# Factors per token spread to rows by way of DRAM instead of by transposes, in a two-layer hybrid encoder trunk

## The chip, the cores and the metric

The kernel runs on one NeuronCore of a Trainium2 chip. The metric is the device time of one execution in microseconds (us). The kernel before takes 1721.14 us, the median of three runs (1721.01 to 1721.66). Its engines are named as in the profile: PE is TensorE's matmul, PEld its weight load, DVE is VectorE, ACT ScalarE, POOL GpSimd, SP the sync engine, which here only issues DMAs.

## The reference

Two residual layers run on a sequence of 512 tokens of width 1024, in float32. Cut to what matters here, one layer is:

```
xn = rms_norm(x, norm1_g)                       # one factor per token
aq, ak, av, bq, bk, bv, cq, ck, cv, cg, gates = split(xn @ w_in)
ya = dilated_mixer(...)      # 6 heads in 3 groups; group outputs weighted by softmax over the
                             # groups' log-denominators: one weight per token, head and group
yb = diff_attention(...)     # 4 heads of 128 values
yb = rms_norm(yb, b_out_norm_g) * (1 - lam_init)          # one factor per token and head
yc = bidirectional_retention(...)                          # 4 heads of 128 values
yc = silu(cg) * rms_norm(yc, c_out_norm_g)                 # one factor per token and head
merged = sum_i sigmoid(gate_i) * (branch_i @ W_branch_i)
x = x + merged @ w_o
h = square(relu(rms_norm(x, norm2_g) @ w_mlp1))            # one factor per token
x = x + h @ w_mlp2
```

Every product with a weight matrix is made in three passes of a 32-bit matmul format: each operand is split into a high and a low part, and high by high, high by low and low by high are added.

## The kernel before, in words

**Layout.** Activations lie feature-major: a tile has 128 features on the partitions and the 512 tokens along the row. Projections to queries, keys and values come out token-major (128 tokens on the partitions, four such blocks, `NJ = 4`). A factor per token is worked out token-major, as a column of a tile of 128 partitions by 4 blocks. To multiply a feature-major tile it has to stand in every partition as a row of 512.

**The stages.** Each layer runs `sequence` (L841): projection waves A, B and C, gates G, branch products W, output products O, and then M1 and M2, the two MLP products. `gemm` (L287) does one chunk of 512 (or 384) output columns in four accumulators `acc0` to `acc3`, one PSUM bank each, with weights that SP fetches (`raw`), ACT rounds (`whi`) and DVE completes (`wlo`), two units ahead of use. Attention, retention and norms run as side threads between the matmuls of the projections. Four more PSUM banks (`pm`) serve all of these.

**The four places where a factor is spread.** (1) `norm_spread` (L423) turns a column broadcast to 128 x 128 through TensorE, four blocks, into a bank `ps_norm`, and ACT copies that to the row tile `rB`. It runs twice a layer. (2) `head_norm` (L579) runs for the four differential heads (branch 1) and the four retention heads (branch 2). It turns the feature-major head `y` to token-major (`ps_yt`, four transposes), ACT squares and sums it, DVE works out the factor `hg` and multiplies (`yn`), and four more transposes bring `yn` back to feature-major in `ps_yb`, from where it is scaled and split. (3) `thread_a` (L709) has the group weights `wt` (`awt`, 24 columns: 3 groups x 2 heads x 4 blocks). For each group DVE copies 8 of them out to 128 x 512 (`wx`), TensorE turns that (`ps_thread_a`), and DVE multiplies the group's output `ya` by the bank.

**What sets the order.** The methods only record operations, in program order. `emit` (L1064) then places them engine by engine by a list schedule of its own: each operation has a reckoned duration, each hand-over a reckoned delay, and the earliest ready one goes first. A DMA from POOL is reckoned as 1.0 us of POOL and 2.0 us until it has landed:

```
d = kb / 290 if name == "SP" else 0.1 if name == "ACT" else 1.0    # L233, in dma()
far = 2.0 if i in self.moves else BEHIND[e]                        # L1168, in emit()
```

On the chip every engine then works through its own instructions strictly in that order and waits where an input has not come. `yield ("wait", "yb")` (L603) and `("wait", "wx")` (L750) hold a side thread back by 8.0 and 1.0 us of reckoned TensorE time while operations are recorded. POOL does nothing else but issue DMAs: it loads the residual `xr` (L958) and stores `xspill` (L1006).

Of the kernel before, what the change touches and what calls it, by code (L numbers as in the profile page):

```python
# [9 lines left out]
FT = mybir.dt.float32  # L10
FR = mybir.dt.float32r
AF = mybir.ActivationFunctionType
OP = mybir.AluOpType
# [3 lines left out]
P = 128  # L17
SEQ = 512
D = 1024
NJ = 4  # L20
# [92 lines left out]
class Trunk:  # L113
# [307 lines left out]
        return r  # L421

    def norm_spread(self, r):  # L423
        b2 = self.ps(name="ps_norm")
        for j in range(NJ):
            self.tr(b2[:, j * P:(j + 1) * P], r[:, j:j + 1].to_broadcast([P, P]), self.ident)
        rB = self.U(name="rB")
        self.act(rB, b2)
        return rB


    def wave_buffers(self, kind):
# [146 lines left out]
    def head_norm(self, l, branch, h, y, s):  # L579
        gain = self.ghead[:, 2 * (branch - 1) + l:2 * (branch - 1) + l + 1]  # L580
        if branch == 2:
            yield ("need", ("cg", l))
        yield ("wait", "y")
        b = self.ps(name="ps_yt")
        for j in range(NJ):
            self.tr(b[:, j * P:(j + 1) * P], y[:, j * P:(j + 1) * P], self.ident)
        ss = self.tiny(4, "yss")
        for j in range(NJ):
            self.act(y[:, j * P:(j + 1) * P], b[:, j * P:(j + 1) * P], AF.Square, accum_out=ss[:, j:j + 1])
        f = self.tiny(4, "hf")  # L590
        if s is not None:
            q = self.tiny(4, "hq")
            s0 = s.rearrange("p (j m) -> p j m", m=2)[:, :, 0]
            self.stt(q, s0, EPS, s0, OP.mult, OP.mult)
            self.stt(f, ss, 1.0 / 128, q, OP.mult, OP.add)
        else:
            self.ts(f, ss, 1.0 / 128, EPS, OP.mult, OP.add)
        g = self.tiny(4, "hg")
        self.rsqrt(g, f)
        yn = self.U(name="yn")  # L600
        self.tt(yn.rearrange("p (j e) -> p j e", j=NJ), b.rearrange("p (j e) -> p j e", j=NJ),
                g[:, :, None].to_broadcast([P, NJ, P]), OP.mult)
        yield ("wait", "yb")  # L603
        b2 = self.ps(name="ps_yb")
        for j in range(NJ):
            self.tr(b2[:, j * P:(j + 1) * P], yn[:, j * P:(j + 1) * P], self.ident)
        out = self.y[l, branch]
        if branch == 1:
            out[h] = self.split(b2, "yn", scale=gain)
        else:  # L610
            self.stt(yn, b2, gain, self.silu[l][h], OP.mult, OP.mult)
            self.silu[l][h] = None
            yield
            out[h] = self.split(yn, "yn")
        if None not in out:
            self.flags.add(("y", l, branch))
        yield
# [91 lines left out]
    def thread_a(self, l):  # L709
        nmx = self.tiny(24, "anm", 2)  # L710
        den = self.tiny(24, "aden", 2)
        ys = []
# [19 lines left out]
        d = self.tiny(24, "ad", 2)  # L732
        for g in range(3):
# [8 lines left out]
        wt = self.tiny(24, "awt", 2)  # L742
        self.tt(wt.rearrange("p (g a) -> p g a", a=8), d.rearrange("p (g a) -> p g a", a=8),
                z1[:, None, :].to_broadcast([P, 3, 8]), OP.mult)
        yield
        for g in range(3):
            wx = self.U((P, NJ, 2, 64), name="wx")
            self.copy(wx, wt[:, g * 8:g * 8 + 8].rearrange("p (m j) -> p j m", j=NJ)[:, :, :, None].to_broadcast(
                [P, NJ, 2, 64]))
            yield ("wait", "wx")  # L750
            b = self.ps(name="ps_thread_a")
            for j in range(NJ):
                self.tr(b[:, j * P:(j + 1) * P], wx[:, j].rearrange("p m d -> p (m d)"), self.ident)
            self.tt(ys[g], ys[g], b, OP.mult)
            yield
            self.y[l, 0].append(self.split(ys[g], "yn"))
            yield
# [461 lines left out]
```

## Time and profile before

| what | value |
|---|---|
| median of 3 runs | 1721.14 us (1721.01 to 1721.66) |
| the profiled execution, its own time | 1721.42 us |
| span, first to last instruction | 1719.6 us |
| PE busy | 1709.5 us, 99% of the span, 8120 matmuls |
| DVE, ACT, POOL busy | 1094.3 (64%), 813.0 (47%), 13.3 us (1%) |
| granted TensorE clock over the span | 1.000 |
| DMA queue of SP, of POOL | 26.0% and 1.0% of the 16 DMA engines' time |

The span leaves 1.8 us of the execution's own time outside. The profile page lists busy time by engine, the granted clock, DMA queues, the chain of work that ended last, and the costliest groups of instructions. A row of a timeline is: start in us, duration in us, engine, line, operation, output<-inputs, shape, count, and in brackets the idle time before it and who ended it. Matmuls overlap, so what one of them costs is read from the distance between starts and not from its duration.

### The profile page before, as it was taken

The numbers are of one execution on the slowest core, as the hardware profiler recorded it, in microseconds if no ns is written. First come the engines' busy times: TensorE is split into PE (matmuls) and PEld (weight loads), VectorE is DVE, ScalarE is ACT, GpSimd is POOL, SyncE is SP. The second block draws the span as 40 slices with busy tenths as digits, with TensorE's granted clock in tenths as the row PEclk, the third lists the DMA queues.
The fourth block names the chain that finished last, engine by engine and source line by source line (L and its number), as shares of the span: only waits on it lengthen the run. The fifth ranks groups of instructions, "written<-read, shape, count | busy, mean of one in ns | idle before, by whom it ended". The sixth has DMA issues, their size and how long they took to land. (4 is left out here: it accounts for less than half of the span.)

```text
span 1719.6 us, 21537 instructions
## 1 busy us (share of the span) xinstructions
PE 1709.5 (99%) x8120; PEld 1454.8 (85%) x8120; DVE 1094.3 (64%) x2126; ACT 813.0 (47%) x1529; POOL 13.3 (1%) x29
## 2 busy tenths in 40 slices
PE   8999999999999999999999999999999999999999
PEld 8889988888888888888898899888888888888887
DVE  8788897887655343434468788888867543434342
ACT  7676674655344232323457666646543441414141
POOL 0000000000000000000000000000000000000000
PEclk9999999999999999999999999999999999999999
DMA  6212212223322222222332222222232222222221
GB/s 222 106 60 72 83 56 95 78 74 105 104 98 98 98 98 98 98 95 93 107 123 86 71 68 78 80 74 86 74 123 90 96 97 98 98 98 98 98 92 68
DMA packets 47960, 160.64 MB, mean 93 GB/s; under 512 B 5616, under 2 KB 6256, under 8 KB 47728
## 3 DMA queue, kind: packets, MB, share of 16 engines
q1 hardware_dynamic: 45072, 151.84, 26.0%
q0 software_dynamic: 1920, 6.29, 1.0%
q8 instruction: 64, 1.05, 0.2%
q10 hardware_dynamic: 864, 1.13, 0.2%
q14 instruction: 40, 0.33, 0.1%
HBM read 155.05 MB, written 4.19 MB: 93 GB/s over the span
## 5 line engine op out<-in xcount | busy, mean ns | idle before, releaser
L185 DVE TENSOR_TENSOR wlo<-raw,whi 128x1024 fp32r<-128x1024 f32 (+2 forms) x297 | 345.0, 1162 | 456.7 <-ACT whi L175 456.0
L175 ACT ACTIVATE whi<-raw 128x1024 fp32r<-128x1024 f32 (+2 forms) x297 | 300.2, 1011 | 629.8 <-PE acc L224 560.7
L224 PE MATMUL acc<-xgh,whi 128*128 128x512 f32 x960 | 377.1, 393 | 0.0
L224 PE MATMUL acc<-xgl,whi 128*128 128x512 f32 x960 | 374.7, 390 | 0.0
L224 PE MATMUL acc<-xgh,wlo 128*128 128x512 f32 x960 | 374.2, 390 | 0.0
L224 PEld LDWEIGHTS acc<-xgh,wlo 128*128 128x128 f32 x960 | 180.3, 188 | 37.6
L224 PEld LDWEIGHTS acc<-xgh,whi 128*128 128x128 f32 x960 | 180.3, 188 | 37.4 <-DVE gate L194 0.8
L224 PEld LDWEIGHTS acc<-xgl,whi 128*128 128x128 f32 x960 | 180.4, 188 | 36.1
L224 PE MATMUL acc<-whi,xgh 128*128 128x384 f32 (+1 forms) x576 | 202.5, 355 | 6.0 <-ACT whi L175 5.5
L224 PE MATMUL acc<-wlo,xgh 128*128 128x384 f32 (+1 forms) x576 | 201.7, 350 | 0.0
L224 PE MATMUL acc<-whi,xgl 128*128 128x384 f32 (+1 forms) x576 | 201.3, 349 | 0.0
L224 PE MATMUL acc<-hh,whi 128*128 128x512 f32 x512 | 199.2, 389 | 0.0
L224 PE MATMUL acc<-hl,whi 128*128 128x512 f32 x512 | 199.2, 389 | 0.0
L224 PE MATMUL acc<-hh,wlo 128*128 128x512 f32 x512 | 199.2, 389 | 0.0
L224 PEld LDWEIGHTS acc<-whi,xgh 128*128 128x128 f32 x576 | 108.8, 189 | 13.0 <-ACT whi L175 5.8
L224 PEld LDWEIGHTS acc<-wlo,xgh 128*128 128x128 f32 x576 | 109.2, 189 | 6.0 <-DVE wlo L185 0.3
L224 PEld LDWEIGHTS acc<-whi,xgl 128*128 128x128 f32 x576 | 109.0, 189 | 5.3
L224 PEld LDWEIGHTS acc<-hl,whi 128*128 128x128 f32 x512 | 96.1, 188 | 20.0
L224 PEld LDWEIGHTS acc<-hh,wlo 128*128 128x128 f32 x512 | 96.1, 188 | 19.9
L224 PEld LDWEIGHTS acc<-hh,whi 128*128 128x128 f32 x512 | 96.1, 188 | 19.9
L175 ACT ACTIVATE qk<-ps_prep 64x512 fp32r<-64x512 f32 (+1 forms) x144 | 69.8, 485 | 20.3 <-DVE qk L185 11.4
L185 DVE TENSOR_TENSOR xr<-xr,acc 128x512 f32<-128x512 f32 (+1 forms) x81 | 54.6, 678 | 30.6 <-PE acc L224 30.1
(199 smaller groups left out, 2225.3 us busy)
## 6 DMA issues: line engine op xcount, KB each, us to landing
raw<-in_weights_dram SPq DMA_DIRECT2D x236, 512.0 KB, 3.2
raw<-in_weights_dram SPq DMA_DIRECT2D x55, 384.0 KB, 3.0
xt<-in_x_dram SPq DMA_DIRECT2D x8, 256.0 KB, 5.1
xr<-in_x_dram POOLq DMA_DIRECT2D x8, 256.0 KB, 3.9
xspill<-xr POOLq DMA_DIRECT2D x8, 256.0 KB, 2.5
xr<-xspill POOLq DMA_DIRECT2D x8, 256.0 KB, 3.5
blob<-in_blob_dram SPq DMA_DIRECT2D x1, 1024.0 KB, 8.4
raw<-in_weights_dram SPq DMA_DIRECT2D x4, 256.0 KB, 2.6
```

Of the source, the lines that this page charges most:

```text
L175: lambda: self.nc.scalar.activation(out, in_, func, **k))
L185: self.dve(out, [out], [a, b], lambda: self.nc.vector.tensor_tensor(out, a, b, op=op))
L224: self.op("PE", d, [out], [lhsT, rhs], lambda: self.nc.tensor.matmul(out, lhsT, rhs, start=start, stop=stop))
```

## The change

A helper `spread` takes a column tile, stores it to a scratch tile in DRAM as rows (a store of `n * 512` single elements of 4 bytes, from POOL's queue), and loads each row from DRAM into all 128 partitions (or two rows into 64 partitions each), again from POOL's queue. `norm_spread` uses it in place of four transposes and ACT's copy. `head_norm` multiplies the feature-major `y`, which it keeps, by the row tile `yr`, so that the four transposes back (`ps_yb`) go; the squares are written to the PSUM bank, since `y` must survive. `thread_a` stores all 24 weight columns at once (6 rows) and loads three tiles `wx` by six loads.

```diff
     def norm_spread(self, r):
-        b2 = self.ps(name="ps_norm")
-        for j in range(NJ):
-            self.tr(b2[:, j * P:(j + 1) * P], r[:, j:j + 1].to_broadcast([P, P]), self.ident)
-        rB = self.U(name="rB")
-        self.act(rB, b2)
-        return rB
+        return self.spread(r, 1, "rB")[0]
+
+    def spread(self, r, n, name, rows=P):
+
+        d = self.dp.tile([n, SEQ], FT, name=self.uid("row"))
+        self.dma(self.nc.gpsimd, d.rearrange("i (j p) -> p (i j)", j=NJ), r, 2)
+        out = []
+        for i in range(0, n, P // rows):
+            t = self.U(name=name)
+            for h in range(P // rows):
+                v = d[i + h]
+                self.dma(self.nc.gpsimd, t[rows * h:rows * h + rows], bass.AP(tensor=v.tensor, offset=v.offset, ap=[[0, rows], [1, SEQ]]), 256)
+            out.append(t)
+        return out
...
         for j in range(NJ):
-            self.act(y[:, j * P:(j + 1) * P], b[:, j * P:(j + 1) * P], AF.Square, accum_out=ss[:, j:j + 1])
+            self.act(b[:, j * P:(j + 1) * P], b[:, j * P:(j + 1) * P], AF.Square, accum_out=ss[:, j:j + 1])
...
-        yn = self.U(name="yn")
-        self.tt(yn.rearrange("p (j e) -> p j e", j=NJ), b.rearrange("p (j e) -> p j e", j=NJ),
-                g[:, :, None].to_broadcast([P, NJ, P]), OP.mult)
+        rows, = self.spread(g, 1, "yr")
         yield ("wait", "yb")
-        b2 = self.ps(name="ps_yb")
-        for j in range(NJ):
-            self.tr(b2[:, j * P:(j + 1) * P], yn[:, j * P:(j + 1) * P], self.ident)
         out = self.y[l, branch]
         if branch == 1:
-            out[h] = self.split(b2, "yn", scale=gain)
+            self.stt(y, y, gain, rows, OP.mult, OP.mult)
         else:
-            self.stt(yn, b2, gain, self.silu[l][h], OP.mult, OP.mult)
+            self.tt(y, y, rows, OP.mult)
+            self.stt(y, y, gain, self.silu[l][h], OP.mult, OP.mult)
             self.silu[l][h] = None
-            yield
-            out[h] = self.split(yn, "yn")
+        yield
+        out[h] = self.split(y, "yn")
...
+        wx = self.spread(wt, 6, "wx", 64)
         yield
         for g in range(3):
-            wx = self.U((P, NJ, 2, 64), name="wx")
-            self.copy(wx, wt[:, g * 8:g * 8 + 8].rearrange("p (m j) -> p j m", j=NJ)[:, :, :, None].to_broadcast(
-                [P, NJ, 2, 64]))
             yield ("wait", "wx")
-            b = self.ps(name="ps_thread_a")
-            for j in range(NJ):
-                self.tr(b[:, j * P:(j + 1) * P], wx[:, j].rearrange("p m d -> p (m d)"), self.ident)
-            self.tt(ys[g], ys[g], b, OP.mult)
+            self.tt(ys[g], ys[g], wx[g], OP.mult)
```

Where `emit` places what, in three places. First VectorE in layer 1, where branch A's weights are applied while a retention wave is projected: `awt` are the weights, `ya` the group outputs, `vl` the eviction of a projection's accumulator `acc`. Before:

```order
L219 COPY wx_1881<-awt_1860 128x512
L194 SCALAR_TENSOR_TENSOR vl_1823<-acc_1824,nr_1503_1595,vh_1822 128x128
L185 TENSOR_TENSOR u_1885<-t_1777,trig 128x512
L194 SCALAR_TENSOR_TENSOR vl_1823<-acc_1825,nr_1503_1595,vh_1822 128x128
L185 TENSOR_TENSOR ya_1689<-ya_1689,ps_thread_a_1867 128x512
L194 SCALAR_TENSOR_TENSOR vl_1823<-acc_1826,nr_1503_1595,vh_1822 128x128
L185 TENSOR_TENSOR o_1886<-t_1777,trig 128x8x32 x2
L185 TENSOR_TENSOR wlo_1879<-raw_1840,whi_1878 128x768
L185 TENSOR_TENSOR ynl_1869<-ya_1689,ynh_1868 128x512
L194 SCALAR_TENSOR_TENSOR vl_1823<-acc_1827,nr_1503_1595,vh_1822 128x128
```

The same place on VectorE now:

```order
L194 SCALAR_TENSOR_TENSOR vl_1821<-acc_1822,nr_1501_1593,vh_1820 128x128
L185 TENSOR_TENSOR o_1885<-o_1885,u_1884 128x512
L194 SCALAR_TENSOR_TENSOR vl_1821<-acc_1823,nr_1501_1593,vh_1820 128x128
L185 TENSOR_TENSOR ya_1687<-ya_1687,wx_1860 128x512
L185 TENSOR_TENSOR wlo_1879<-raw_1838,whi_1878 128x768
L194 SCALAR_TENSOR_TENSOR vl_1821<-acc_1824,nr_1501_1593,vh_1820 128x128
L185 TENSOR_TENSOR ynl_1869<-ya_1687,ynh_1868 128x512
L194 SCALAR_TENSOR_TENSOR vl_1821<-acc_1825,nr_1501_1593,vh_1820 128x128
L185 TENSOR_TENSOR ya_1767<-ya_1767,wx_1861 128x512
```

The first `ya` stands at the same place, between the second and the third of the four evictions, and now waits for a tile that a DMA fills; two evictions stand behind it. Second, POOL's queue in layer 1 at branch A and the first heads. Before, these rows follow each other:

```order
L234 DMA xspill<-xr_1141 128x512
L234 DMA xspill<-xr_1142 128x512
L234 DMA xr_2523<-xspill 128x512
L234 DMA xr_2524<-xspill 128x512
L234 DMA xr_2525<-xspill 128x512
```

Now there stands between the last `xspill` and the first `xr`, as its first part:

```order
L234 DMA row_1631<-nr_1501_1593 128x4x1
L234 DMA rB_1632<-row_1631 128x512
L234 DMA row_1859<-awt_1858 128x24x1
L234 DMA wx_1860<-row_1859 64x512
L234 DMA wx_1861<-row_1859 64x512
L234 DMA wx_1862<-row_1859 64x512
L234 DMA wx_1860<-row_1859 64x512
L234 DMA wx_1861<-row_1859 64x512
L234 DMA wx_1862<-row_1859 64x512
L234 DMA row_2137<-hg_2133 128x4x1
L234 DMA yr_2138<-row_2137 128x512
```

Each `row` is a store of a column tile, each tile after it a load of that row; the first `wx` tile is complete with the fourth of the six loads. POOL has 54 more DMAs than before over the program: 22 stores and 32 loads. Third, VectorE at the third differential head of layer 0 (`hg` the head's factor, `y` the head). Before, where the token-major `yn` is made at once and the head comes back through the bank `ps_yb`:

```order
L194 SCALAR_TENSOR_TENSOR hg_1018<-rt_929_1021,hg_1018 128x4
L185 TENSOR_TENSOR yn_1022<-ps_yt_1014,hg_1018 128x512
L185 TENSOR_TENSOR gate_1025<-acc_957,rB_216 128x512
L185 TENSOR_TENSOR wTl_1028<-ps_to_keys_1026,wTh_1027 128x512
L185 TENSOR_TENSOR wlo_1034<-raw_973,whi_1033 128x1024
L194 SCALAR_TENSOR_TENSOR ynl_1038<-ps_yb_1036,ghead,ynh_1037 128x512
```

Now, from the last step of the factor to the multiplication:

```order
L194 SCALAR_TENSOR_TENSOR hg_1017<-rt_928_1020,hg_1017 128x4
L185 TENSOR_TENSOR gate_1024<-acc_955,rB_216 128x512
L185 TENSOR_TENSOR wTl_1027<-ps_to_keys_1025,wTh_1026 128x512
L185 TENSOR_TENSOR wlo_1033<-raw_961,whi_1032 128x1024
L185 TENSOR_TENSOR wTl_1037<-ps_to_keys_1035,wTh_1036 128x512
L185 TENSOR_TENSOR wTl_1042<-ps_to_keys_1040,wTh_1041 128x512
L194 SCALAR_TENSOR_TENSOR y_1008<-y_1008,ghead,yr_1022 128x512
```

Five instructions now stand between the factor and its use, while a store and a load go out and back.

## Rows read from the trace of the kernel before

**Rows 1.** The page: busy time by engine; and span and granted clock of the core.
```profile
PE 1709.5 (99%) x8120; PEld 1454.8 (85%) x8120; DVE 1094.3 (64%) x2126; ACT 813.0 (47%) x1529; POOL 13.3 (1%) x29
core 0: 1719.6 us, clock 1.000
```

**Rows 2.** Who TensorE waited for: us in total, times, longest us.
```profile
PE acc L224 <- ACT whi L175: 5.5, 1, 5.5
PE acc L224 <- DVE v L194: 0.5, 1, 0.5
PE ps_c_head L224 <- ACT wTh L175: 0.3, 1, 0.3
```

**Rows 3.** Timeline of PE around one group of four transposes back.
```profile
1295.31 0.39 PE L224 MATMUL acc<-xgh,wlo 128*128 128x512 f32 x1
1295.54 0.60 PE L228 MATMUL ps_yb<-eye,yn 128*128 128x128 f32 x4
1295.89 0.48 PE L224 MATMUL acc<-xgh,whi 128*128 128x512 f32 x1
1296.21 0.40 PE L224 MATMUL acc<-xgl,whi 128*128 128x512 f32 x1
1296.44 0.40 PE L224 MATMUL acc<-xgh,wlo 128*128 128x512 f32 x1
```

**Rows 4.** The removed instructions by tile: duration ns min/median/max, first and last start.
```profile
L228 PE MATMUL ps_yb<-eye,yn x64: 270/272/273, 302.2 to 1295.9; 128*128 128x128 f32 x64
L228 PE MATMUL ps_norm<-eye,nr x16: 270/272/273, 46.9 to 1383.9; 128*128 128x128 f32 x16
L228 PE MATMUL ps_thread_a<-eye,wx x24: 270/272/273, 161.4 to 1024.6; 128*128 128x128 f32 x24
L175 ACT ACTIVATE rB<-ps_norm x4: 577/580/580, 47.9 to 1384.5; 128x512 f32<-128x512 f32 x4
L219 DVE COPY wx<-awt x6: 409/420/429, 154.9 to 1021.6; 128x512 f32<-128x512 f32 x6
```

**Rows 5.** DMA issues: tile, queue, count, KB each, median us to landing.
```profile
xr<-xspill POOLq DMA_DIRECT2D x8, 256.0 KB, 3.5
xspill<-xr POOLq DMA_DIRECT2D x8, 256.0 KB, 2.5
eye<-in_blob_dram ACTq DMA_DIRECT2D x1, 64.0 KB, 3.2
gcol<-in_cols_dram ACTq DMA_DIRECT2D x1, 18.0 KB, 3.0
```

**Rows 6.** The stores of POOL by tile: time that POOL is busy with one, ns.
```profile
L234 POOL DMA_DIRECT2D xspill<-xr x8: 539/540/544, 837.9 to 864.1; - x8
```

**Rows 7.** Timeline of DVE in layer 1, from branch A's weights to their use.
```profile
1007.54 0.18 DVE L185 TENSOR_TENSOR awt<-ad,az 128x24 f32<-128x24 f32 x1
...
1016.90 0.35 DVE L194 SCALAR_TENSOR_TENSOR vl<-acc,nr,vh 128x128 fp32r<-128x128 f32 x1
1017.17 0.68 DVE L185 TENSOR_TENSOR ya<-ya,ps_thread_a 128x512 f32<-128x512 f32 x1
1017.77 0.34 DVE L194 SCALAR_TENSOR_TENSOR vl<-acc,nr,vh 128x128 fp32r<-128x128 f32 x1
...
1020.16 0.35 DVE L194 SCALAR_TENSOR_TENSOR vl<-acc,nr,vh 128x128 fp32r<-128x128 f32 x1
```

**Rows 8.** Timeline of PEld just behind the last of these rows.
```profile
1020.57 0.19 PEld L224 LDWEIGHTS acc<-whi,xgh 128*128 128x128 f32 x1 [0.25 <-DVE vl L194]
```

**Rows 9.** Timeline of DVE in layer 0, the stage that applies the weights.
```profile
174.51 0.69 DVE L185 TENSOR_TENSOR wTl<-sd,wTh 128x512 fp32r<-128x512 f32 x1
179.14 0.68 DVE L185 TENSOR_TENSOR wTl<-sd,wTh 128x512 fp32r<-128x512 f32 x1
```

**Rows 10.** Timeline of PE beside it: the first use of each of the two.
```profile
178.42 0.40 PE L224 MATMUL ps_c_head<-wTl,vh 128*128 128x512 f32 x1
181.08 0.39 PE L224 MATMUL ps_c_head<-wTl,vh 128*128 128x512 f32 x1
```

**Rows 11.** Busy time by stretch: us, PE, PEld, DVE, ACT, POOL, PEclk, DMA share, GB/s.
```profile
989.00:1161.00 172.00, 171.95 (x877) 151.40 (x877) 146.83 (x329) 105.06 (x234) 0.00 (x0) 1.00 0.24 75
```

## The prediction

> **What bounds the kernel now.** I read the page's busy times first, then TensorE's waits, then its timeline. TensorE is busy for 1709.5 of 1719.6 us at a granted clock of 1.000 [rows 1], and over the whole span it waited for another engine three times, 6.3 us in all, 5.5 of them at one place [rows 2]. So the end is set by the sum of TensorE's work, not by a chain through other engines. What leaves TensorE's queue comes off the time one for one; what is taken off VectorE or ScalarE is worth nothing. But the trace shows no waits only because the builder's own schedule places each instruction just behind its inputs: in layer 1 a weight load for a fresh accumulator sits idle for 0.25 us until VectorE's eviction `vl` ends [rows 8]. An engine that falls behind there stops TensorE at once. VectorE is busy for 146.8 of the 172.0 us of that stage [rows 11].
>
> **What goes from TensorE.** The groups of four transposes that go are 16 in `ps_yb`, 4 in `ps_norm` and 6 in `ps_thread_a`: 64 + 16 + 24 = 104 instructions [rows 4]. The price of a group is read from starts. From the matmul ahead of it to its own start is 0.23 us, the ordinary distance; from its start to the next matmul 0.35 us; and that matmul's own distance to the following one is 0.32 instead of 0.23 [rows 3]. So a transpose costs 0.35 / 4 = 0.087 us, and each return from transposes to matmuls 0.09 us more. In TensorE's order such returns fall from 97 to 82, since some removed groups stood beside other transposes. The gain is 104 x 0.087 + 15 x 0.09 = 9.05 + 1.35 = 10.4 us. On the other engines four `rB` copies of 0.58 us (ScalarE) and six `wx` copies of 0.42 us (VectorE) go [rows 4]; both engines have idle time, so I count nothing for them. The number of VectorE passes over a head stays the same.
>
> **What is added: a round trip per factor.** POOL issues 22 stores and 32 loads more. POOL is busy for 13.3 us [rows 1] and every issue takes it 0.54 us [rows 6], so the queue has room. What counts is the length of a trip, since VectorE, which works in order, waits for its end, and behind the waiting instruction stand evictions and the low parts of weights.
>
> A load of 256 KB from scratch lands 3.5 us after its issue [rows 5]. The store is the unknown: it consists of single 4-byte elements, 512 for a norm or head factor, 3072 for branch A's weights, and no row shows such a store. The nearest is `xspill`, 128 pieces in 2.5 us [rows 5], of which POOL is busy for 0.54 [rows 6]; so 1.96 us pass behind the issue. Two ends for it: the number of pieces costs nothing (2.5 us), or POOL's time grows in proportion to it, 4 x 0.54 + 1.96 = 4.1 us for 512 pieces and 24 x 0.54 + 1.96 = 14.9 us for 3072. (If the whole 2.5 us grew so, A's store would take 60 us; but loads of 128 pieces of 512 and of 144 bytes take 3.2 and 3.0 us [rows 5], so most of a landing is not work on pieces.) I take the middle: half of the 0.54 is fixed, half grows. That gives 0.27 + 4 x 0.27 + 1.96 = 3.3 us and 0.27 + 24 x 0.27 + 1.96 = 8.7 us.
>
> The Trainium skill speaks on both sides here. "DMA: Bandwidth & Descriptors", section "Anatomy of one DMA — SWDGE (gpsimd) path", gives a fixed 2.0 us plus bytes at 436 GB/s and says that many descriptors can go out before their cost shows; by it even A's 12 KB takes an estimated 2.03 us and the sum is 1711.0 us. The same page's "Rules for kernel authors" warns that a strided last dimension becomes one descriptor per element and should be rearranged, which is what this store has and speaks for the rival of 1728.6 us below. No row of this trace decides between the two.
>
> *Heads and norms.* A trip is store + load + two hand-overs of some 0.1 us (the weight load of [rows 8] starts 0.06 us after `vl` ends): 3.3 + 3.5 + 0.2 = 7.0 us. The time that the schedule leaves for it I count in the emitted stream, as the TensorE work that stands between the factor's last instruction and its use, matmuls at 0.227 us for 512 columns [rows 3]. It is 8.2, 9.3, 8.8 and 8.2 us for the retention heads, 6.7, 6.7, 6.0 and 7.0 us for the differential heads, 8.9 us for the norm ahead of M1, and over 90 us for the other norm. So VectorE waits 0.3, 0.3 and 1.0 us at three heads of a layer. Counted in the same way, the first TensorE instruction that needs something queued behind these has 0.7, 1.1 and 10 us to spare. Cost: nothing. If a trip takes 7.8 us (the store at 4.1), the waits are 1.1, 1.1, 1.8 and 0.8 us against 0.7, 1.1, 10 and 3.2: 0.4 us per layer, 0.8 in all. The norm ahead of M1 stays covered.
>
> *Branch A's weights.* The first `wx` tile is complete with the fourth load, so the trip is W + 3 x 0.54 + 3.5 + 0.2 = W + 5.3 us, with W the store. In layer 1, VectorE now gets from `awt` to `ya` in 9.5 us (1007.7 to 1017.2) [rows 7] without a pause to speak of; in the new order it does about as much before `ya`, and the stream holds 10.3 us of TensorE work. I take 10, so VectorE waits W - 4.7. Behind `ya` stand two `vl` evictions whose accumulators the next wave needs with 0.2 us to spare, as the last `vl` does now [rows 7, 8]. TensorE loses W - 4.9. In layer 0 the stream holds 11.5 us and VectorE's rows add up to about 11; I take 11, so the wait is W - 5.7. There no eviction stands behind it; the first to be missed is a `wTl`, which now has 178.42 - 175.20 = 3.2 us and 181.08 - 179.82 = 1.3 us to spare [rows 9, 10], and 2.4 us in the new stream. TensorE loses W - 8.1. With W = 8.7: 3.8 + 0.6 = 4.4 us.
>
> **Sum.** The profiled execution took 1721.42 us, 0.28 above the median of the runs, which is nothing here. 1721.4 - 10.4 + 4.4 = 1715.4 us: the transposes' gain less two waits at branch A, nearly all in layer 1.
>
> **Rivals.**
> 1. *Everything is hidden.* Pieces cost nothing, W = 2.5, the trip for A is 7.8 us against 10 and 11: 1721.4 - 10.4 = 1711.0 us. For it: the near-equal landings of 144-byte and 512-byte pieces. Against: those are 128 pieces, not 3072.
> 2. *A's store eats the gain (the other side).* POOL's time grows with the pieces, W = 14.9. VectorE waits 10.2 us in layer 1 and 9.2 in layer 0, TensorE loses 10.0 + 6.8 + 0.8 for the heads = 17.6 us: 1728.6 us. It decides from W = 11.4, where 2W - 13.0 + 0.6 reaches 10.4. For it: one row, 0.54 us for 128 pieces, is all there is on the price of a piece. Beyond it, W = 60 would add about 107 us (1818 us); I give this little.
> 3. *The new order brings its own waits.* `emit` re-places thousands of rows around the gaps. The schedule before left 6.3 us of waits, 5.5 of them at the start; if the new one hits a few places where reckoned and real times differ, most of 10 us goes: about 1721 us. Against: the one before met real times almost everywhere.
>
> **How the numbers follow.** The forecast (W between 5.5 and 10.5, 1711.6 to 1719 us) gets 0.40, the first rival 0.18, the second 0.27 and its far end 0.03, the third 0.12. About 0.2% (3.4 us) is what a measurement of this kernel can tell from no change. Faster by more than that: 0.36 of the forecast and all 0.18 of the first rival = 0.54. Within it: 0.04 of the forecast, 0.04 of the second rival's lower part and 0.08 of the third = 0.16. Slower: the remaining 0.30. The range runs from the first rival, less 0.5 us, to just past the second: 1710.5 to 1731 us. It leaves out the far end and a better packed order.
>
> **What would show it.** Right: TensorE's busy time near 1699 us with 8016 matmuls; a wait of TensorE of about 4 us for a `vl` in layer 1's branch A stage, with VectorE idle ahead of `ya` for about 4 us, ended by a `wx` load; head factors `yr` waited for by 1 us at most. A POOL row of 512 pieces of about 1.3 us, and of 3072 pieces of about 6.8 us, shows the middle price; 0.54 us for both the first rival; 2.2 and 13 us the second. Wrong: waits of TensorE behind many heads, which would mean that loads or hand-overs are longer than rows 5 say, or waits that no `wx`, `yr` or `rB` row precedes, which would be the third rival.

## The result, and the profile after

The changed kernel takes 1861.58 us (median of 4 runs, 1860.99 to 1863.13) against 1721.08 us (4 runs, 1720.92 to 1721.66): a ratio of 1.0818 with a 95% interval of 1.0801 to 1.0835. It is 140.5 us slower. The forecast was 1715.4 us with a range up to 1731. The profiled execution took 1862.05 us and has a span of 1860.3 us.

The page of the changed kernel, busy time by engine, and the core's span and granted clock; both answer to [rows 1]:

```profile
PE 1731.5 (93%) x8016; PEld 1467.9 (79%) x8016; DVE 1092.2 (59%) x2120; ACT 814.2 (44%) x1525; POOL 48.6 (3%) x83
core 0: 1860.3 us, clock 0.963
```

The 104 matmuls that should go are gone (8016 of 8120). Still TensorE is busy for 22.0 us longer, and its idle time within the span has grown from 1719.6 - 1709.5 = 10.1 to 1860.3 - 1731.5 = 128.8 us. These two make the 140.7 us by which the span is longer. Busy time grew although work went, because the granted clock over the span is 0.963 where it was 1.000. Whom TensorE now waits for, as in [rows 2] (total us, times, longest):

```profile
PE acc L224 <- DVE gate L185: 43.9, 4, 16.5
PE acc L224 <- DVE vl L194: 30.7, 3, 13.3
PE acc L224 <- DVE gate L194: 15.9, 2, 8.1
PE ps_yt L228 <- ACT y L175: 13.2, 2, 6.6
PE acc L224 <- DVE rl L194: 9.7, 2, 5.2
```

Nothing of this size but the one wait at the start stood in [rows 2]. All but one row names VectorE. VectorE in turn, in the same view, waited for DMAs from the scratch rows:

```profile
DVE y L194 <- DMA yr<-row: 74.8, 8, 11.8
DVE y L185 <- DMA yr<-row: 33.0, 6, 10.6
DVE ya L185 <- DMA wx<-row: 24.6, 2, 13.5
DVE rl L194 <- DMA rB<-row: 14.7, 2, 7.7
```

That is 147 us at 18 places: the heads (`yr`), branch A (`wx`) and the norm ahead of M1 (`rB`). The DMA issues, as in [rows 5] (last number: median us from issue to landing), and the time that POOL is busy with a store, as in [rows 6] (ns, min/median/max):

```profile
row<-hg POOLq DMA_DIRECT2D x16, 2.0 KB, 9.5
row<-awt POOLq DMA_DIRECT2D x2, 12.0 KB, 16.7
yr<-row POOLq DMA_DIRECT2D x16, 256.0 KB, 5.3
```

```profile
L234 POOL DMA_DIRECT2D row<-hg x16: 760/765/816, 294.6 to 1417.0; - x16
L234 POOL DMA_DIRECT2D row<-awt x2: 1436/1440/1443, 154.6 to 1073.6; - x2
```

A store of 2 KB lands after 9.5 us, and only 0.765 of them are POOL's. From 512 to 3072 pieces POOL's time grows by 0.675 us, which is 0.26 ns for a piece. Most of the landing lies behind the issue.

One place in full, the retention heads of layer 0. POOL's timeline (in brackets: idle time before, and who ended it; where an engine is named there that had nothing to give, as `ps_b_scores` here, the wait was for the store's landing):

```profile
294.60 0.82 POOL L234 DMA_DIRECT2D row<-hg  x1 [119.47 <-DVE hg L194]
304.28 0.55 POOL L234 DMA_DIRECT2D yr<-row  x1 [8.87 <-PE ps_b_scores L224]
304.82 1.51 POOL L234 DMA_DIRECT2D row<-hg  x2
315.01 1.16 POOL L234 DMA_DIRECT2D yr<-row  x2 [8.68 <-DMA row<-hg]
```

VectorE's timeline there:

```profile
301.59 0.16 DVE L194 SCALAR_TENSOR_TENSOR hg<-rt,hg 128x4 f32<-128x4 f32 x1
313.50 0.69 DVE L185 TENSOR_TENSOR y<-y,yr 128x512 f32<-128x512 f32 x1 [10.57 <-DMA yr<-row]
325.70 0.69 DVE L185 TENSOR_TENSOR y<-y,yr 128x512 f32<-128x512 f32 x1 [5.13 <-DMA yr<-row]
332.52 1.88 DVE L185 TENSOR_TENSOR gate<-acc,rB 128x512 f32<-128x512 f32 x3
```

And TensorE's:

```profile
333.36 0.66 PE L224 MATMUL acc<-whi,xgh 128*128 128x384 f32 x1 [16.30 <-DVE gate L185]
```

The store of the first head at 294.60 lands after 9.2 us, and its load is issued 9.7 us after it. The factors of the next two heads are ready by 301.8, but their stores stand behind that load in POOL's order and start at 304.82; their loads start at 315.01. VectorE stops for 10.57 us at the first `y`, and for 5.13 more at a later one. The evictions `gate` stand behind these in its order, and TensorE, which needs their accumulators, stands still for 16.3 us. What that does to the clock (view by stretch, columns as in [rows 11]):

```profile
304.00:314.00 10.00, 10.00 (x48) 8.26 (x47) 0.50 (x1) 0.85 (x1) 2.05 (x3) 1.00 0.33 88
324.00:330.00 6.00, 0.00 (x0) 0.00 (x0) 3.85 (x6) 0.63 (x1) 0.54 (x1) 0.50 0.63 104
335.00:340.00 5.00, 5.00 (x21) 4.60 (x21) 3.27 (x5) 1.47 (x4) 0.00 (x0) 0.71 0.35 120
340.00:350.00 10.00, 10.00 (x60) 9.39 (x59) 7.71 (x16) 6.34 (x14) 0.00 (x0) 1.00 0.14 54
```

TensorE stands still from 317.05 to 333.36. The granted clock is 1.00 (2.4 GHz) in the stretch of work ahead of that, 0.50 (1.2 GHz) from 324 to 330, within the wait, on average still 0.71 from 335 to 340, when TensorE is at work again, and 1.00 from 340 on. So such a wait is paid twice: once as idle time, and again as work at a lower clock.

### The profile page after: what moved, and what is told of

Read it like the earlier page. It is cut to its first block, busy times and chain, and to the rows that moved or that the text cites. A ratio compares the mean times of both kernels' runs of the same rounds, so it can differ in the third digit from the quotient of the medians.

```text
span 1860.3 us, 21436 instructions
## 1 busy us (share of the span) xinstructions
PE 1731.5 (93%) x8016; PEld 1467.9 (79%) x8016; DVE 1092.2 (59%) x2120; ACT 814.2 (44%) x1525; POOL 48.6 (3%) x83
## 5 line engine op out<-in xcount | busy, mean ns | idle before, releaser
L224 PE MATMUL acc<-xgh,whi 128*128 128x512 f32 x960 | 383.2, 399 | 25.6 <-DVE gate L194 15.9
L224 PE MATMUL acc<-xgl,whi 128*128 128x512 f32 x960 | 379.2, 395 | 0.0
L224 PE MATMUL acc<-xgh,wlo 128*128 128x512 f32 x960 | 378.4, 394 | 0.0
L224 PEld LDWEIGHTS acc<-xgh,whi 128*128 128x128 f32 x960 | 183.7, 191 | 64.8 <-DVE gate L194 16.7
L224 PE MATMUL acc<-ynh,whi 128*128 128x512 f32 x176 | 73.7, 419 | 28.4 <-DVE vl L194 17.3
L175 ACT ACTIVATE qk<-ps_prep 64x512 fp32r<-64x512 f32 (+1 forms) x144 | 69.9, 485 | 24.6 <-DVE qk L185 14.4
```

The source lines that it names most:

```text
L175: lambda: self.nc.scalar.activation(out, in_, func, **k))
L224: self.op("PE", d, [out], [lhsT, rhs], lambda: self.nc.tensor.matmul(out, lhsT, rhs, start=start, stop=stop))
```

## The experiments

The theory after this result was that the length of the trip alone does it, the store's landing above all (TRIP). Its main rival was that the re-placed order brings the waits (ORDER). Within the store, the rivals were the number of pieces, the size of a piece, the queue, and where the pieces lie.

**1. What makes a small store land late.** Kernel before, with unneeded DMAs added in the MLP stages, where POOL is free; nothing waits for the stores.

```diff
+ p_dense: dma(gpsimd, d.rearrange("i (j p) -> p (i j)"), col)     # 512 x 4 bytes side by side, as the change
+ p_stepc: the same 512 pieces, 64 bytes apart     p_stepf: 512 bytes apart
+ p_runs:  128 x 16 bytes     p_runl: 128 x 96 bytes     p_alla: 3072 x 4 bytes
+ p_actq:  p_dense from ScalarE's queue     p_col: 128 x 4 bytes side by side     p_whole: one row of 2 KB in 16 pieces
+ q_bcsame: one 2 KB row into 128 partitions     q_bcmany: 128 rows
```

> The kernel before, with extra DMAs in the MLP stages of each layer whose results nothing needs (the output is unchanged): stores to DRAM of 512 elements of 4 bytes side by side as in the change (p_dense), the same 512 each 64 bytes apart (p_stepc) and 512 bytes apart (p_stepf), 128 pieces of 16 bytes (p_runs), one row of 2 KB in 16 pieces (p_whole), 3072 elements of 4 bytes as for branch A (p_alla), 128 pieces of 96 bytes (p_runl), 128 elements of 4 bytes (p_col), the 512 elements from ScalarE's queue instead of POOL's (p_actq); and loads of 128 rows of 2 KB, all of one row (q_bcsame) and of 128 rows (q_bcmany). Theory LINE (small writes into the same stretch of DRAM wait for one another): p_dense lands after 9.5 us as in the changed kernel, p_stepc and p_stepf after 2.5 to 4, p_runs after about 4, p_actq like p_dense. Theory COUNT (each piece costs, wherever it goes): p_stepc and p_stepf 9.5 as p_dense, p_runs and p_col about 4, p_alla 16.7. Theory SMALL (any write of less than some size is acknowledged late, however many there are): all of p_dense, p_stepc, p_stepf, p_runs, p_col about 9, p_whole 2.5. Theory QUEUE (POOL's queue is slow, not the store): p_actq about 3, the rest of POOL's all alike. For the loads: q_bcsame 5.3 and q_bcmany 3.5 if reading one row 128 times is what made the changed kernel's loads slow. Time of the program: within 2 us of 1721.

The run took 1721.11 us. Its DMA issues:

```profile
q_bcsame<-p_bcset POOLq DMA_DIRECT2D x2, 256.0 KB, 3.7
p_dense<-prb POOLq DMA_DIRECT2D x2, 2.0 KB, 9.3
p_stepc<-prb POOLq DMA_DIRECT2D x2, 2.0 KB, 2.2
p_runs<-prb POOLq DMA_DIRECT2D x2, 2.0 KB, 1.8
p_alla<-prb POOLq DMA_DIRECT2D x2, 12.0 KB, 15.6
p_actq<-prb ACTq DMA_DIRECT2D x2, 2.0 KB, 9.2
```

Each figure is the median of two DMAs of one execution. The same 512 pieces land after 9.3 us side by side and after 2.2 us when they lie 64 (or 512) bytes apart. So it is not their number, their size or POOL's queue. The DMA packets say the same: in `p_dense` and in `p_stepc` all 16 data packets start 1.4 to 1.9 us after the issue and none takes longer than 0.20 us. The data goes out alike; what comes late is the end of the writes. (`p_whole`, one row from one partition, lands after 3.4 us; why it takes longer than `p_runs` wasn't followed up.) Reading one row 128 times (3.7 us) is no slower than reading 128 rows (4.1 us).

**2. How near is too near.** Again unneeded stores in the kernel before.

```diff
+ p_cola, p_colb, p_colc, p_cold: 128 x 4 bytes at a step of 4, 8, 16, 32 bytes
+ p_half, p_dense, p_two, p_four: 256, 512, 1024, 2048 pieces of 4 bytes side by side
+ p_own: 512 x 4 bytes side by side, in the order of the partitions
```

> The kernel before with more unneeded stores in the MLP stages (output unchanged), each of 4-byte pieces to DRAM. 128 pieces, one per partition: side by side (p_cola, 16 in a stretch of 64 bytes), 8 bytes apart (p_colb, 8 in 64), 16 apart (p_colc, 4 in 64), 32 apart (p_cold, 2 in 64). 256, 512, 1024 and 2048 pieces in dense rows of the change's layout (p_half, p_dense, p_two, p_four). And 512 dense pieces in the order of the partitions, so that 64 bytes come from four neighbouring partitions (p_own). Theory PIECES (writes that fall into the same 64 bytes wait for one another): p_cola 7.8, p_colb about 4, p_colc about 3, p_cold about 2; p_own 9.3 like p_dense; p_half near 8.5. Theory SHARED (a stretch is slow when several DMA engines write into it, and the pieces of one engine are merged): p_own about 2; p_colc and p_cold about 2, since four neighbouring partitions belong to one engine; p_colb in between; p_cola 7.8. In both the time rises slowly with the number of rows: p_two near 10.7, p_four near 13, between 9.3 for one row and 15.6 for six. Program: within 2 us of 1721.

The run took 1720.59 us:

```profile
p_own<-prb POOLq DMA_DIRECT2D x2, 2.0 KB, 8.0
p_cola<-prb POOLq DMA_DIRECT2D x2, 0.5 KB, 8.8
p_colb<-prb POOLq DMA_DIRECT2D x2, 0.5 KB, 3.4
p_colc<-prb POOLq DMA_DIRECT2D x2, 0.5 KB, 1.7
p_four<-prb POOLq DMA_DIRECT2D x2, 8.0 KB, 10.3
```

With 16, 8 and 4 pieces in each 64 bytes a store lands after 8.8, 3.4 and 1.7 us (the same 128 pieces side by side took 7.8 in the first run), and from 128 to 2048 pieces the landing grows only from 8.8 to 10.3 us. That fits writes into one small stretch of DRAM that wait for one another while different stretches go on side by side; no run looks into the memory itself. How wide a stretch is (64 bytes or less) these steps don't settle; at a step of 16 bytes PIECES said about 3 us, and the 1.7 measured are no later than at 32 bytes (1.8). Why 3072 pieces take 15.6 us where 2048 take 10.3 stays open too. SHARED falls: in `p_own` only four neighbouring partitions write into 64 bytes, and a single one into 16, and it lands after 8.0 us.

**3. The parts one by one.** The heads alone, branch A alone, the norms alone; the other places keep their transposes.

```diff
 p2: before.py with the new head_norm and spread
 p3: before.py with the new thread_a and spread
 p4: before.py with the new norm_spread
```

> The change at the head norms alone (16 trips; norm_spread and branch A as before). Theory TRIP (VectorE waits for a store of 9.5 us plus a load of 5.3 us, 15.0 us in all, where the schedule leaves 6.0 to 9.3): TensorE gains 64 transposes, about 6 us, and loses about 80 to 90 us of waits plus some 25 us at a lower granted clock: 1805 to 1835 us, every wait of TensorE with a wait of VectorE for a yr load ahead of it. Theory ORDER (the new order of instructions is worse in itself, whatever the trips take): the loss goes with the number of moved instructions and is about a third of the 140 us, 1760 to 1775, with waits not preceded by a yr load.

> The change at branch A's weights alone (2 trips). Theory TRIP: a store of 16.7 us, loads of 1.6 + 3.1 us, 21.6 us against 10 and 11 left by the schedule, so VectorE waits 11 to 13 us in each layer; TensorE loses 11 in layer 1 and 8 in layer 0, plus some clock, and gains 2 us: 1735 to 1747 us. Theory ORDER: about a third of the 140 us, 1760 to 1775.

> The change at norm_spread alone (4 trips; 2 of them have over 90 us). Theory TRIP: at the norm ahead of M1 a trip of about 15 us against 8.9 us left; VectorE waits 6 to 7 us there in each layer, TensorE 4 to 5, less 1.4 us gained, plus some clock: 1727 to 1735 us. Theory ORDER: 1750 or more.

| part | time, us | ratio (95% interval) | span against before, us | TensorE idle against before, us | VectorE's waits for rows, us |
|---|---|---|---|---|---|
| heads | 1825.77 | 1.0611 (1.058 to 1.0641) | +104.7 | +87.5 | 105.0 |
| branch A | 1742.49 | 1.0127 (1.0097 to 1.0156) | +20.5 | +16.6 | 21.7 |
| norms | 1731.44 | 1.0067 (1.0044 to 1.009) | +9.9 | +8.9 | 13.4 |

The spans add up to 135.1 of the 140.7 us of the whole change, though each part alone re-places the instructions in another way. All three times lie in TRIP's ranges and outside ORDER's. TRIP holds.

**4. Only the layout of the rows in DRAM.** The whole change, but each partition writes its four factors as one piece of 16 bytes. The row then has another order, so VectorE reads it at a step of 16 bytes.

```diff
-        self.dma(gpsimd, d.rearrange("i (j p) -> p (i j)", j=NJ), r, 2)
+        self.dma(gpsimd, d.rearrange("i (p j) -> p i j", j=NJ), r.rearrange("p (i j) -> p i j", j=NJ), 2)
...
-            out.append(t)
+            out.append(t.rearrange("q (p j) -> q j p", j=NJ))
```

> The whole change, but the store has each partition's four block factors side by side (128 pieces of 16 bytes for a norm or head, 768 for branch A), and the multiplications read the row through a permuted view. Theory STORE (the slow acknowledgement of the 4-byte stores is the cause): the store lands in 1.8 us as the probe did, the load in 3.7 to 5.3, a trip takes 5.7 to 7.3 us against the 6.0 to 9.3 that the schedule leaves and branch A's about 7 against 10 and 11; nearly all waits of TensorE go, the 10.4 us of transposes remain: 1710 to 1716 us. Theory LOADS (the loads of the changed kernel are slow by themselves, 5.3 us and up to 10.1): waits of 1 to 3 us at most heads stay, 1722 to 1740. A third: VectorE reads the permuted row (a step of 16 bytes) at a lower rate; its multiplications with yr, rB and wx then take over 0.75 instead of 0.69 us.

Measured: 1717.9 us (1716.62 to 1719.65), ratio 0.9981 (0.9972 to 0.9991). Page and DMA issues of this run, and from its costliest groups one in the changed kernel (second last) and here (last; count, then busy us and mean ns):

```profile
PE 1697.7 (99%) x8016; PEld 1442.7 (84%) x8016; DVE 1140.4 (66%) x2120; ACT 815.3 (48%) x1525; POOL 42.8 (2%) x83
row<-hg POOLq DMA_DIRECT2D x16, 2.0 KB, 1.7
yr<-row POOLq DMA_DIRECT2D x16, 256.0 KB, 4.2
```

```profile
L194 DVE SCALAR_TENSOR_TENSOR rl<-acc,rB 128x512 f32<-128x512 f32 x64 | 43.7, 685 | 15.1 <-DMA rB<-row 14.7
```

```profile
L194 DVE SCALAR_TENSOR_TENSOR rl<-acc,rB 128x512 f32<-128x512 f32 x64 | 66.9, 1065 | 0.0
```

A different order of the rows in DRAM gives back 143.7 us. By operation and tile, each engine runs its instructions here in the same order as in the changed kernel, so the order has no part in these 143.7 us, and ORDER falls. The landing falls from 9.5 to 1.7 us, and TensorE is busy for 1697.7 us at a clock of 1.000, 11.8 us less than before. The time is 1.9 us above STORE's range, and the third expectation came true, VectorE's slower reads: a multiplication that reads its row at a step of 16 bytes takes 1.065 us instead of 0.685, and over all such reads its busy time is 48 us longer.

**5. Does it help to tell the builder?** The trips are reckoned at measured lengths instead of 1.0 + 2.0 us: with the 4-byte stores (p7), and with the 16-byte pieces (p8).

```diff
- store, load: 1.0 us of POOL, 2.0 us until landed
+ p7: store 0.8 and 8.9 (branch A 1.45 and 15.3), load 0.55 and 4.8 (2.7)
+ p8: store 0.55 and 1.4 (branch A 0.8 and 1.4), load 0.55 and 4.0 (2.7)
```

> The whole change with its 4-byte stores, but the builder reckons with the measured trips: 0.8 + 8.9 us for a store and 0.55 + 4.8 for a load, for branch A 1.45 + 15.3 and 0.55 + 2.7 (instead of 1.0 + 2.0 each). It moves the uses of the rows later and nothing else. Theory LATENESS (TensorE loses because uses stand ahead of their rows in VectorE's order, not because the rows are needed so early): heads and branch A cost nothing any more; the norm ahead of M1 cannot be moved and keeps 5 to 7 us per layer: 1718 to 1728 us. Theory NEED (the branch products need the heads soon, so TensorE waits whatever the order): 1760 or more.

> 16-byte pieces and a reckoning with the trip that goes with them (store 0.55 + 1.4, load 0.55 + 4.0, branch A's store 0.8 + 1.4 and its loads 0.55 + 2.7). Theory STORE and LATENESS together: TensorE waits hardly more than before, 1710 to 1713 us, at or a little below the one with 16-byte pieces alone. If the loads vary (3.7 to 10 us as in the changed kernel), 1714 to 1725.

p7 took 1758.05 us, ratio 1.0213 (1.0193 to 1.0234): 103.5 us better than the change, but not near the kernel before. While several such stores are under way, their neighbours are late too: `yr` loads land after 4.7 to 17.3 us (median 6.8), and packets of 4096 bytes on POOL's queue take up to 8.1 us, 0.159 as a rule. SP's weights are held up as well: in the changed kernel their packets of 4096 bytes take up to 9.2 us, in the kernel before at most 1.3 and in p6 2.1. So a trip has no fixed length that a builder could reckon with. p8 took 1726.53 us, ratio 1.0029 (1.002 to 1.0039), 8.6 us worse than without the reckoning. Both expectations were missed: p7 lies between its two ranges, p8 1.5 us above its upper one. For p8 the first suspect was VectorE's slow reads, which the reckoning takes for fast ones.

**6. Rows put back in order, and the queue.** With 16-byte pieces, ScalarE copies each norm's row back into plain order once, so that only 22 slow reads are left (p9); the same with the reckoning of p8 (p10); norms by transposes as before, heads and branch A by 16-byte pieces (p11).

```diff
     def norm_spread(self, r):
+        rows = self.spread(r, 1, "rq")[0]
+        rB = self.U(name="rB")
+        self.act(self.by(rB), rows)
+        return rB
```

> The whole change with 16-byte pieces as in the run that took 1717.9 us, except that each norm's row is put back into plain order once by a ScalarE copy (four instructions), so that the 112 to 128 multiplications by it read plain rows again; heads and branch A keep the reads at a step of 16 bytes (22 instructions). READ theory (what is left above 1711 us in that run are VectorE's slow reads, 1.07 against 0.69 us, about 48 us of VectorE): VectorE's busy time falls from 1140 to about 1100 us, TensorE's waits fall from about 7 to 2 or 3 us beside the one at the start, and the time is 1712 to 1715 us. TRIP theory (what is left are landings of loads, 4 to 6 us): VectorE's waits for yr stay near 9 us and the time stays within 1 us of 1717.9.

> The same, and the builder reckons each store at 0.55 us and 1.4 us until it has landed, each load at 0.55 and 4.0 (branch A 0.8 and 1.4, 0.55 and 2.7). Earlier this reckoning with slow reads everywhere gave 1726.5 us, 8.6 more than without it. READ theory (VectorE's slow reads, which the reckoning holds for fast, made that excess): now within 2 us of the run without the reckoning, about 1711 to 1715 us. LATER theory (to place the uses later is bad in itself, as it moves other work): again 5 us or more above the run without it, 1718 us or more.

> Heads and branch A by 16-byte pieces, the norms by transposes as in the kernel before (16 transposes and four copies stay, no norm row goes to DRAM). The transposes cost about 16 x 0.087 + returns = 1.4 to 1.7 us of TensorE. READ theory: VectorE near 1100 us; 1713 to 1717 us, so 1 to 2 us above the version with a repacked norm row unless that one's norm trips are waited for (xr loads and rB on POOL's queue). TRIP theory: near 1718 us.

p9: 1714.68 us (1714.04 to 1715.7), ratio 0.9964 (0.9951 to 0.9978). p11: 1717.58 us, ratio 0.998 (0.9971 to 0.9989). VectorE is at 1099.3 us in p9, and READ is right on the time there, 3.2 us less than p6. It isn't right on the waits: TensorE's, beside the one at the start, are 6.3 us where 2 to 3 were expected (8.1 in p6), and VectorE's for `yr` don't fall (11.1, 9.3 in p6), as TRIP said. p11 lies just above READ's range, though VectorE is at 1099.8 there: TensorE's idle time is 16.0 us (15.4 in p9, 17.7 in p6), and the 16 transposes it keeps make it 2.5 us busier than p9, not 1.4 to 1.7. p10: 1724.12 us, ratio 1.0019 (1.001 to 1.0028); the slow reads were not p8's trouble. In p10's timeline of POOL, at the retention heads of layer 0, one sees another:

```profile
292.71 0.54 POOL L234 DMA_DIRECT2D yr<-row  x1 [2.30 <-ACT ps_yt L175]
293.24 0.54 POOL L234 DMA_DIRECT2D row<-hg  x1
298.04 0.54 POOL L234 DMA_DIRECT2D yr<-row  x1 [4.26 <-issue]
298.58 0.54 POOL L234 DMA_DIRECT2D row<-hg  x1
```

Each store follows at once on a load that waited for its own store, 2.3 and 4.3 us: POOL's order strings the heads' trips together. These two stores start 1.4 and 2.3 us after their factors are ready, and, issued right behind a load of 256 KB, they land only after 4.3 and 4.9 us, where the median of this run's stores is 1.8. Three runs take the stores off POOL's queue: the changed kernel with its 4-byte stores (p12), p9 (p13) and p10 (p14). In each of them the builder places the order anew, on VectorE in 24 to 45 places, so queue and order change together; it reckons a store on ScalarE's queue at 0.1 us of ScalarE in p12 and p13 and at 0.4 in p14, where the traces have 0.33 to 0.38.

```diff
-        self.dma(self.nc.gpsimd, d.rearrange(...), r, 2)
+        self.dma(self.nc.scalar, d.rearrange(...), r, 2)
```

> The changed kernel with its 4-byte stores as they are, but issued from ScalarE's queue; the loads stay on POOL's. A store then never stands behind a load that waits for an earlier store. POOL-QUEUE theory (the trips of heads that follow one another are strung together by POOL's order, which makes waits of 10 to 13 us out of 6 to 7): the four retention heads' stores of layer 0 start at their factors' times, TensorE's idle time falls by 25 to 45 us and the time to 1815 to 1840 us. STORE theory (dense stores in flight hold each other and the loads up whichever queue issues them): stores start early but land after 10 to 17 us, loads wait as long as before, and the time stays between 1845 and 1870 us.

> The version with 16-byte pieces and a repacked norm row (1714.7 us), with its stores issued from ScalarE's queue and the loads left on POOL's. POOL-QUEUE theory (a store that stands behind a waiting load is what is left): the stores start within 0.5 us of their factors, VectorE's waits for yr fall from 11 us to under 6, and the time is 1711.5 to 1713.5 us. LENGTH theory (store 1.7 plus load 4.1 us is simply longer than what the schedule leaves): the waits stay at 8 us or more and the time within 1 us of 1714.7; if ScalarE's issues (about 0.4 us each) and its own waits for a factor cost something, above that, up to 1718.

> The same stores from ScalarE's queue in the version that reckons trips at their measured length (1724.1 us with the stores on POOL's). POOL-QUEUE theory (that version lost its time because the reckoned order put stores behind loads that wait 2 to 5 us): 1712 to 1716 us, no wait of TensorE for gate above 2 us. LATER theory (placing uses later moves other work to bad places): 1720 us or more, and the two waits for gate of about 4 us stay.

p12: 1870.33 us, ratio 1.0868 (1.0849 to 1.0888), 8.8 us worse than the change and just past the end of STORE's range. ScalarE's queue in p12 and POOL's queue behind it:

```profile
298.48 0.37 ACTq L234 DMA_DIRECT2D row<-hg  x1
303.67 0.37 ACTq L234 DMA_DIRECT2D row<-hg  x1
306.19 0.37 ACTq L234 DMA_DIRECT2D row<-hg  x1
```

```profile
308.23 0.57 POOL L234 DMA_DIRECT2D yr<-row  x1 [135.74 <-PE ps_b_scores L224]
318.67 1.07 POOL L234 DMA_DIRECT2D yr<-row  x2 [9.86 <-DMA row<-hg]
```

The second store is issued in good time at 303.67, and yet it lands only after 14.4 us and its load starts 15.0 us after it. So a dense 4-byte store can be held up by others from ScalarE's queue too, as the STORE theory said, and taking POOL's order away doesn't give back the 140 us. It isn't any neighbour that does it: in the run with the heads alone, two such stores 0.75 us apart on POOL's queue land after 9.8 and 9.3 us. The Trainium skill, "DMA: Bandwidth & Descriptors", section "Queues, rings and completion order", says that the signal of a DMA's end is written only after every earlier write of the same DMA engine, across its queues. The `yr` load issued at 308.23 behind the second and third store agrees with that rule: it lands after 13.0 us, at 321.26, when those stores have landed at 318.12 and 318.29. The rule doesn't cover the second store's own 14.4 us, since the one store ahead of it had landed at 307.69, and no run takes the rule apart from the memory itself.

p13: 1720.98 us, ratio 1.0006 (0.9996 to 1.0015), above what either theory expected; VectorE's waits for `yr` stay at 11.9 us, as LENGTH said. p14: 1713.71 us (1713.23 to 1713.83), ratio 0.9956 (0.9944 to 0.9969), within what POOL-QUEUE said. Page and waits of p14:

```profile
PE 1698.1 (99%) x8016; PEld 1443.3 (84%) x8016; DVE 1099.7 (64%) x2120; ACT 818.9 (48%) x1529; POOL 30.2 (2%) x61
PE acc L224 <- DVE gate L185: 2.5, 2, 1.3
DVE y L194 <- DMA yr<-row: 1.6, 3, 0.8
```

Against p10, where TensorE waited 7.9 us for `gate`, moving the stores is worth 10.4 us; against p9 the same move costs 6.3. So here the true length in the reckoning and the stores' own queue only pay together. A reading that fits, and that these runs don't isolate: the reckoning puts each use where its row lands if the trip starts on time, and POOL's queue kept trips from that; at the same heads p14's stores land after 1.4 to 2.1 us. Why p13 is as slow as it is stays open (TensorE's waits for `vl` rise from 2.4 to 4.8 us, its idle time from 15.4 to 20.0). p14 has the lowest time, 7.4 us under the kernel before, but only 1.0 under p9, and the intervals of the two ratios overlap.

## Why the prediction was wrong

**The gain was right.** Forecast were 10.4 us and a busy TensorE near 1699. At a clock of 1.000 p6, p9 and p14 show 1697.7 to 1698.1, so 11.4 to 11.8 us.

**The step that failed is the store's landing.** The prediction said "half of the 0.54 is fixed, half grows", which gave 3.3 us for 512 pieces and 8.7 for 3072; measured are 9.5 and 16.7. With that, "Cost: nothing" for heads and norms became 104.7 and 9.9 us of span, and the 4.4 us for branch A 20.5. Both its ends for the 512 pieces (2.5 and 4.1 us) lay under half of the truth. The mistake is in the kind of cost: it counted pieces as work of POOL, and the pieces' place in DRAM sets the landing (9.3 us side by side, 2.2 at a step of 64 bytes). POOL's rows of 0.765 and 1.44 us are nearer to the first rival's 0.54 than to the 1.3 and 6.8 of the middle, so the prediction's own sign would have pointed to "everything is hidden": POOL's time told nothing of the landing. The rows it leaned on [rows 5] have pieces of 2048, 512 and 144 bytes, each longer than the 64 bytes at which the delay was already gone; such rows could not show it. The Trainium skill's fixed 2.0 us and bytes over 436 GB/s ("DMA: Bandwidth & Descriptors", "Anatomy of one DMA — SWDGE (gpsimd) path") come within 0.3 us of the 1.8 us for 16-byte pieces, and are off by 7 us for the same 2 KB in 4-byte pieces. The warning of the Trainium skill on the same page, section "Rules for kernel authors", to rearrange what becomes one descriptor per element, was the right advice here, 143.7 us in p6, though `p_stepc` shows that the number of pieces isn't what cost the time.

**The load was taken too short.** 3.5 us were forecast; it landed after 5.3 in the changed kernel, and after 4.1 to 4.2 in p6 and p9. The trace before already had loads of 256 KB from POOL's queue at 3.9 us (`xr<-in_x_dram`), which [rows 5] leave out.

**The arithmetic behind the landing holds in the sum, and there partly by luck.** With the landings of the run with the heads alone, 9.4 + 4.6 + 0.2 = 14.2 us against the times that the schedule was counted to leave gives 22.3 us of waiting for the retention heads and 30.4 for the differential heads of a layer, 105.4 in both layers; measured 105.0. But the parts are off by 10 us each way, 44.6 counted against 34.5 for the retention heads and 60.8 against 70.5 for the differential heads:

```profile
DVE y L194 <- DMA yr<-row: 70.5, 8, 11.7
DVE y L185 <- DMA yr<-row: 34.5, 8, 10.5
```

The first row is the differential heads. The retention heads follow one another within a few microseconds: in layer 0 their waits are 10.5, 0.3, 3.2 and 2.7 us, so a wait at one can serve the next as well, which a sum of single trips leaves out. Why the differential heads wait longer than counted stays open. For branch A with W = 15.6 the forecast's terms W - 4.9 and W - 8.1 give 10.7 us in layer 1 and 7.5 in layer 0; TensorE waited 12.4 and 4.4, and again the sum is nearer than its parts. For the norm ahead of M1, 9.4 + 5.0 + 0.2 - 8.9 = 5.7 us a layer; measured 6.7.

**Two things were left out.** First the clock: it fell to 0.50 within the wait of 16.3 us shown above, and TensorE took up work again below 1.00. Busy time is 1731.5 - 1697.7 = 33.8 us longer than in p6 with the same matmuls in the same order at a clock of 1.000, a quarter of the loss. Second POOL's own order: the prediction named VectorE's queue behind a waiting instruction but not POOL's, where the next head's store stands behind a waiting load. In the changed kernel that isn't decisive (p12); with 16-byte pieces and true reckoning, moving the stores and placing the order anew gave 10.4 us.

**The rivals.** The second pointed at the right term, the price of the store, and its 14.9 us for branch A are near the measured 16.7; but that is luck, since it takes them from POOL's time (13 us, measured 1.44), and it puts the heads, which carry three quarters of the loss, at 0.8 us. The first comes near what a well-laid store gives, 1711.0 against 1713.71. The third, the order, has no part in the loss (p6); p9, p10, p13 and p14, which differ in queue, reckoning and order, lie within 10.4 us of one another. Waits behind many heads, which the prediction named as a sign of longer loads or hand-overs, came mostly from the store, 6.2 us longer than forecast against 1.8 for the load.

## What to carry to other kernels

What a small store costs can lie in where its writes land, and not in what the issuing engine spends on it: when a column of 4-byte values goes to DRAM, let each partition write its values as one piece of 16 bytes or more, and put the order right on the reading side, once for a row that many instructions read. To reckon a round trip at its measured length, or to keep the next store off the queue of a waiting load, cost time here when done alone (8.6 to 9.4 and 6.3 us) and gave 1.0 us when done together. Before a trip takes the place of a few transposes (0.35 us a group here), a side measurement of the very pattern says more than a row of a smoother one.

## What the runs showed of the hardware

- 4-byte writes side by side in DRAM end late: 8.8 us for 128 of them, 3.4 at a step of 8 bytes, 1.7 at 16. POOL's time (0.54 us for 128 pieces, 0.77 for 512) and that of the packets of such a store of 512 (at most 0.21 us) show nothing of it.
- They hold up others: while such stores were under way, packets of 4096 bytes took up to 8.1 us on POOL's queue (p7) and 9.2 on SP's (the changed kernel), 0.159 as a rule.
- A 16-byte-piece store issued right behind a load of 256 KB on POOL's queue landed after 4.3 to 5.1 us (p10), against 1.8 as a rule.
- VectorE's multiplication with one float32 operand at a step of 16 bytes: 1.065 us for 128x512 against 0.685. The Trainium skill, "SBUF — State Buffer", section "Door 1: The DMA port swizzle", tells of lines of 16 bytes, with a penalty for every access that crosses to a new one; at this step every access does, and the rows agree.
- TensorE's granted clock, 1.000 over the whole span before [rows 1], was 0.50 within a wait of 16.3 us, 0.71 on average from 335 to 340 us after work had begun again at 333.36, and 1.00 from 340 on.
